# Partial sums of exponentials in a two-layer attention trunk: two tiles a head instead of four, one group of ones products for both heads

## The chip, the cores and the metric

The kernel runs on one core of a Trainium2 chip. The metric is the device time of one execution in microseconds (us); lower is better. The core has five engines that the profile names by short names: PE (TensorE, matrix products; PEld is its loading of weights), DVE (VectorE), ACT (ScalarE), POOL (GpSimd) and SP (SyncE, which issues the DMAs). Every engine works through its own queue in order, and semaphores make one engine wait for another.

## The reference, cut to what matters

There are two layers. Each projects a normalised input (1024 latent tokens and 256 context tokens, 1024 features), runs attention and a linear recurrence side by side, and merges the two. The change is in the attention:

```python
def gqa(q, k, v):
    s = jnp.einsum('bqkgd,bskd->bkgqs', q, k).astype(jnp.float32)
    p = jax.nn.softmax(s, axis=-1).astype(v.dtype)
    return jnp.einsum('bkgqs,bskd->bqkgd', p, v)
...
    k_all = jnp.concatenate([k_c, k_l], axis=1)
    v_all = jnp.concatenate([v_c, v_l], axis=1)
    o_lat = latent_attention(q_l, k_all, v_all)
...
    if need_ctx:
        o_ctx = gqa(q_c.reshape(B, L, N_KV_HEADS, Q_PER_KV, HEAD_DIM), k_c, v_c).reshape(B, L, D_ATTN)
```

There are 16 query heads of 64 features. A latent query sees all 1280 keys, a context query only the 256 context keys. Layer 0 needs the context rows too, layer 1 doesn't. The softmax's denominator, the sum of the exponentials over the keys, is what the changed lines compute.

## The kernel before

Activations lie with features on the 128 partitions and tokens along the row. Tokens come in three chunks: L0 and L1 of 512 latent tokens, C of 256 context tokens. A product in full precision is split: each operand is a high part (fp32r) and the rest, and three fast products stand for one.

The attention of a layer is cut into **units**. A tile `t` of 0 to 7 holds two heads. For each tile there are four latent units, (L0, head 0), (L0, head 1), (L1, head 0), (L1, head 1), and in layer 0 a fifth, C, which takes both heads at once (256 queries each). A latent unit has 512 queries and ten key tiles (`kt`) of 128 keys, a context unit two. So there are 32 latent units in each layer and 8 context units in layer 0. In a unit:

- `s1` multiplies queries by keys once for the row maxima; VectorE reduces each result (`mp`, line 979).
- `s2`, for each key tile, makes the scores again, transposed (keys on the partitions), with the maximum subtracted by an extra row. ScalarE takes the exponential twice, as fp32 (`pf`, line 1006) and as fp32r (`ph`, line 1007). VectorE makes the rest `pl = pf - ph` (line 1008), which reads two tiles in SBUF.
- `add` sums the `pf` tiles on GpSimd into partial tiles `acc` (lines 1019, 1022, 1024). The ten key tiles of a latent unit make four partial tiles, by the groups (0,1,2), (3,4,5), (6,7), (8,9). The first member of a group needs no instruction, so a latent unit has six additions. A context unit copies its two tiles into two partial tiles.
- `av` multiplies `ph` and `pl` by the values (`avps`).
- `lsum` multiplies the partial tiles by a tile of ones that is 32 columns wide (`lps`). Product x fills partitions 32x to 32x+31 of one bank. ScalarE copies the bank (`lrow`), and one DMA writes one row of each product to DRAM (`ls`).
- `recip`, after the second head, reads the partial sums of both heads back from DRAM spread over 128 partitions, adds them on VectorE (lines 1080 and 1082, `rq`), takes the reciprocal, and sends it through DRAM to the partitions where `done` scales the output.

`acc` has five buffers, `pf` three, `pl` four. The bank that `s1`, `s2`, `lps` and the fills use is one of six.

PE's order is the order in which the Python code calls `mm`. A clock of the builder, `tl.now`, grows with every product by its supposed cost, and the steps of the units are due at times of that clock: the list of steps is stretched over the time that the units (`cost`) and the **fills** (`fcost`) are supposed to take. Fills are the projections for the gates (`gps`), which run between the steps of the units, so that PE has work while the other engines make exponentials. A supposed cost only moves steps against each other in the order; nothing waits for the builder's clock on the chip. The other engines' orders follow from the same calls.

The ones products in fp32 are two instructions each in the trace, so that a group of four counts eight. The rows of the acc additions in the trace bear the lines 1022 (second member of a group) and 1024 (later ones).

Of the kernel before, what the change touches and what calls it, by code (L numbers as in the profile page):

```python
# [100 lines left out]
def trunk_kernel(ctx: ExitStack, tc: tile.TileContext, xT, cc, par, wmod, win, wgate, wo,  # L101
# [446 lines left out]
    def layer_dram(l):  # L548
# [7 lines left out]
        d["ls"] = {(t, c): dtile(l, f"ls{t}{c}", [4, 512] if c == "C" else [2, 4, 512]) for t in range(8) for c in och}  # L556
# [152 lines left out]
    for l in range(DEPTH):  # L709
# [206 lines left out]
        with tc.tile_pool(name="att", bufs=2, reuse_waits="tile") as work:  # L916
# [21 lines left out]
            zt = {}  # L938

            class Unit:  # L940


                def __init__(self, i, t, c, e, g0):
# [14 lines left out]
                    add(g0 + self.nkt + (5.0 if e == 2 else 3.6), self.lsum)  # L958
                    self.groups = ((0,), (1,)) if e == 2 else ((0, 1, 2), (3, 4, 5), (6, 7), (8, 9))
                    self.accs = {}  # L960
# [51 lines left out]
                def add(self, kt, pf):  # L1012

                    x = next(x for x, g in enumerate(self.groups) if kt in g)
                    at = self.groups[x].index(kt)
                    if at == 0:
                        self.accs[x] = pf
                        if self.e == 2:
                            G.tensor_scalar(self.acc_tile(x), pf, 1.0, 0.0, op0=OP.mult, op1=OP.add)
                    elif at == 1:  # L1020
                        first = self.accs[x]
                        G.tensor_add(self.acc_tile(x), first, pf)  # L1022
                    else:
                        G.tensor_add(self.accs[x], self.accs[x], pf)  # L1024

                def acc_tile(self, x):
                    self.accs[x] = work.tile([128, 512], F32, name="acc", tag="acc", bufs=5)
                    return self.accs[x]
# [21 lines left out]
                def lsum(self):  # L1050

                    lp = ptile("s", "lps")
                    ng = len(self.groups)
                    for x in range(ng):
                        mm(lp[32 * x:32 * x + 32], ones32, self.accs[x], True, True, 0.9 / ng)
                    row = sm("lrow")
                    S.activation(row[0:32 * ng], lp[0:32 * ng], AF.Copy)
                    ls = dd["ls"][self.t, self.c]
                    dst = ls if self.e == 2 else ls[self.e]
                    tl.at(1.2, lambda: DMA.dma_start(dst[0:ng], row[0:32 * ng:32]), True)  # L1060
                    if self.e:
                        tl.at(5.0, self.recip, True)

                def recip(self):
# [4 lines left out]
                    rq = const.tile([128, 40], F32, name="rq", tag="rq", bufs=2)  # L1069
# [8 lines left out]
                    def back():  # L1078
                        r = rq[:, 32:32 + x]
                        V.tensor_add(r, rs[:, 0], rs[:, 1])  # L1080
                        for y in range(2, ng):
                            V.tensor_add(r, r, rs[:, y])
# [258 lines left out]
```

## Time and profile before

| what | value |
|---|---|
| median of three runs | 3177.37 us |
| the profiled execution | 3176.29 us, span 3174.5 us, mean granted clock 0.984 |
| PE | 3049.5 us busy, 96% of the span |
| DVE | 2453.9 us, 77% |
| ACT | 1715.0 us, 54% |
| POOL | 1024.5 us, 32% |
| attention of layer 0 | from 598.9 to 1320.7 us of the span: 721.8 us |
| attention of layer 1 | from 2237.9 to 2882.6 us: 644.7 us |

The two stretches of attention run from the first `s1` product of a layer to the end of its last `lps` product. The busy time of PE is the union of modelled product times; since products are pipelined, one that is shown as 0.39 us long can be followed by the next after 0.23 us. The start of the next product tells what one costs.

### The profile page before, as it was taken

To read this page: it belongs to the slowest core of one execution; us is meant where nothing else is said; L and a number is where in the kernel's file an instruction comes from. 1 tells how busy PE (TensorE), PEld (TensorE's weight loads), DVE (VectorE), ACT (ScalarE), POOL (GpSimd) and SP (SyncE) were. 2 spreads that over 40 slices of the span, in tenths; PEclk is the share of its full clock that TensorE was granted. 3 is DMA by queue.
4 is the path that set the end of the run, shared out by engine and by line. 5 is a ranking of instruction groups with operands and counts; after the bars stand their busy time and mean duration, and the time that the engine had idled before them with its cause. 6 is when DMAs were issued, how large, how long until landed. Compare 5 with 4: busy or idle time off the path is not lost.

```text
span 3174.5 us, 42428 instructions
## 1 busy us (share of the span) xinstructions
PE 3049.5 (96%) x14592; PEld 2459.1 (77%) x14592; DVE 2453.9 (77%) x3675; ACT 1715.0 (54%) x3060; POOL 1024.5 (32%) x777
## 2 busy tenths in 40 slices
PE   7999999999999999999999999999999999999999
PEld 3788778788777777887777778777777777777887
DVE  7665887589989998556685776897799989996544
ACT  4323767466666666445654324676476666663222
POOL 0211444134334434245522222333244444441000
PEclk9999999999999999999999999999999999999999
DMA  5443111421222222254555452111412121115554
GB/s 197 145 149 126 44 57 50 125 63 54 76 68 82 60 62 75 97 189 158 170 196 175 135 176 71 58 47 53 123 55 76 58 75 58 55 58 173 183 173 140
DMA packets 243416, 332.08 MB, mean 105 GB/s; under 512 B 63664, under 2 KB 109552, under 8 KB 242944
## 3 DMA queue, kind: packets, MB, share of 16 engines
q1 hardware_dynamic: 243200, 329.37, 32.6%
q8 instruction: 115, 1.88, 0.2%
q14 instruction: 101, 0.83, 0.1%
HBM read 252.54 MB, written 76.58 MB: 104 GB/s over the span
## 4 chain that ended last, share of the span: by engine, by line
PE 53%; DVE 19%; issue 6%; ACT 4%; DMA 4%; POOL 3%; SPq 0%; DVEq 0%; POOLq 0%; ACTq 0%
PE gps L145 29%; PE avps L145 8%; PE s2ps L145 7%; PE s1ps L145 4%; DVE pl L1008 3%; DVE wlo L227 3%; DVE mp L979 2%; PE lps L145 2%; POOL macc L360 2%; PE gtps L145 1%; DVE ti L856 1%; PE qps L145 1%; POOL b L853 1%; DVE g L867 1%; PE vps L145 1%
## 5 line engine op out<-in xcount | busy, mean ns | idle before, releaser
L145 PE MATMUL gps<-h,whi 128*128 128x512 f32 x3328 | 1042.3, 394 | 18.3 <-DVE g L876 15.9
L145 PEld LDWEIGHTS gps<-h,whi 128*128 128x128 f32 x3328 | 613.5, 190 | 135.3 <-issue 10.7
L1008 DVE TENSOR_TENSOR pl<-pf,ph 128x512 fp32r<-128x512 f32 x656 | 627.2, 957 | 71.3 <-ACT ph L1007 67.9
L145 PE MATMUL gps<-h,wlo 128*128 128x512 f32 x1664 | 655.2, 394 | 1.4 <-DVE wlo L227 1.4
L1006 ACT ACTIVATE pf<-s2ps 128x512 f32<-128x512 f32 x656 | 392.9, 599 | 343.1 <-PE s2ps L145 171.7
L1022 POOL TENSOR_TENSOR acc<-pf 128x512 f32<-128x512 f32 x256 | 353.0, 1379 | 686.4 <-ACT pf L1006 686.2
L979 DVE TENSOR_REDUCE mp<-s1ps 128x1 f32<-128x512 f32 (+1 forms) x800 | 453.7, 584 | 59.9 <-PE s1ps L145 56.5
L1007 ACT ACTIVATE ph<-s2ps 128x512 fp32r<-128x512 f32 x656 | 390.0, 595 | 0.0
L227 DVE TENSOR_TENSOR wlo<-wraw,whi 128x512 fp32r<-128x512 f32 x392 | 330.8, 865 | 62.2 <-ACT whi L226 33.0
L226 ACT ACTIVATE whi<-wraw 128x512 fp32r<-128x512 f32 x324 | 194.6, 628 | 340.9 <-PE gps L145 269.1
L145 PEld LDWEIGHTS gps<-h,wlo 128*128 128x128 f32 x1664 | 314.3, 189 | 71.4 <-DVE wlo L227 2.2
L145 PE MATMUL s1ps<-k,qa 128*128 128x512 f32 (+1 forms) x800 | 287.3, 368 | 15.9 <-DMA qa<-q0L 10.7
L145 PEld LDWEIGHTS s1ps<-k,qa 128*128 128x128 f32 x800 | 244.5, 310 | 55.4 <-DVE mp L979 10.6
L145 PE MATMUL avps<-pl,vv 128*128 128x512 f32 x656 | 262.4, 400 | 8.0 <-DVE pl L1008 7.7
L145 PE MATMUL avps<-ph,vv 128*128 128x512 f32 x656 | 266.2, 406 | 0.0
L145 PE MATMUL s2ps<-qa,k 128*128 128x512 f32 x656 | 260.8, 398 | 4.4 <-DVE mp L979 3.4
L145 PE MATMUL s2ps<-qb,k 65*128 65x512 f32 x656 | 262.5, 400 | 0.1
L145 PE MATMUL gps<-e,whi 128*128 128x512 f32 x768 | 244.8, 399 | 0.4 <-DVE e L227 0.2
L360 POOL TENSOR_TENSOR macc<-macc,wmt 128x512 f32<-128x512 f32 x112 | 156.6, 1398 | 252.3 <-ACT wmt L358 228.0
L1024 POOL TENSOR_TENSOR acc<-acc,pf 128x512 f32<-128x512 f32 x128 | 183.1, 1430 | 79.4 <-ACT pf L1006 77.4
L145 PE MATMUL qps<-h,whi 128*128 128x512 f32 x640 | 203.6, 399 | 1.7 <-DVE h L674 0.9
L145 PE MATMUL gps<-c,whi 128*128 128x256 f32 x1024 | 197.8, 289 | 2.7 <-DVE c L222 1.9
(214 smaller groups left out, 4945.0 us busy)
## 6 DMA issues: line engine op xcount, KB each, us to landing
wraw<-in_win_dram SPq DMA_DIRECT2D x200, 256.0 KB
wraw<-in_wo_dram SPq DMA_DIRECT2D x192, 256.0 KB
wm<-in_wmod_dram SPq DMA_DIRECT2D x32, 512.0 KB
wm<-in_wmod_dram SPq DMA_DIRECT2D x8, 1024.0 KB
rb<-rq SPq DMA_DIRECT2D x64, 128.0 KB
k<-k SPq DMA_DIRECT2D x24, 320.0 KB
v<-vst SPq DMA_DIRECT2D x20, 256.0 KB
vv<-v SPq DMA_DIRECT2D x8, 640.0 KB
```

Source lines behind the costliest of these rows:

```text
L145: nc.tensor.matmul(o, a, b, start=start, stop=stop)
L226: S.activation(dst_hi, src, AF.Copy)
L227: (V if lo_eng == "v" else G).tensor_sub(dst_lo, src, r32(dst_hi))
L360: G.tensor_add(acc, acc, t)
L853: G.tensor_mul(a2, a2, ti)
L856: V.tensor_tensor_scan(h, a, a2, 0.0, op0=OP.mult, op1=OP.add)
L979: tl.at(0.3, lambda: V.reduce_max(self.mp[:, j, b:b + 1], ps[:, :n], axis=AX.X))
L1006: S.activation(pf, ps, AF.Exp)
L1007: S.activation(ph, ps, AF.Exp)
L1008: tl.at(1.4, lambda: V.tensor_sub(pl, pf, r32(ph)))
L1022: G.tensor_add(self.acc_tile(x), first, pf)
L1024: G.tensor_add(self.accs[x], self.accs[x], pf)
```

## The change

A latent unit now has two partial tiles, by the groups (0,1,2,3,4) and (5,6,7,8,9), so it has eight additions on GpSimd instead of six. The partial tiles of head 0 are kept until head 1 has made its own, and one `lsum` after head 1 multiplies all four by ones: one group of four products, one `lrow`, one DMA to DRAM for the two heads of a tile and chunk. A context unit adds its two tiles into one partial tile and makes one product. `recip` adds two rows of partial sums for each head instead of four; for a context unit there is nothing to add. The builder's clock counts 1.1 for a group (before 0.9) and 0.58 for each latent unit in `cost` (before 0.9).

```diff
-        d["ls"] = {(t, c): dtile(l, f"ls{t}{c}", [4, 512] if c == "C" else [2, 4, 512]) ...}
+        d["ls"] = {(t, c): dtile(l, f"ls{t}{c}", [1, 512] if c == "C" else [4, 512]) ...}
...
-                    add(g0 + self.nkt + (5.0 if e == 2 else 3.6), self.lsum)
-                    self.groups = ((0,), (1,)) if e == 2 else ((0, 1, 2), (3, 4, 5), (6, 7), (8, 9))
-                    self.accs = {}
+                    if e:
+                        add(g0 + self.nkt + (5.0 if e == 2 else 3.6), self.lsum)
+                    self.groups = ((0, 1),) if e == 2 else ((0, 1, 2, 3, 4), (5, 6, 7, 8, 9))
+                    if e != 1:
+                        sums[t, c] = []
+                    self.sums, self.acc = sums[t, c], None
...
-                    x = next(x for x, g in enumerate(self.groups) if kt in g)
-                    at = self.groups[x].index(kt)
+                    at = next(g.index(kt) for g in self.groups if kt in g)
                     if at == 0:
-                        self.accs[x] = pf
-                        if self.e == 2:
-                            G.tensor_scalar(self.acc_tile(x), pf, 1.0, 0.0, op0=OP.mult, op1=OP.add)
+                        self.acc = pf
                     elif at == 1:
-                        first = self.accs[x]
-                        G.tensor_add(self.acc_tile(x), first, pf)
+                        first = self.acc
+                        self.acc = work.tile([128, 512], F32, name="acc", tag="acc", bufs=5)
+                        G.tensor_add(self.acc, first, pf)
+                        self.sums.append(self.acc)
                     else:
-                        G.tensor_add(self.accs[x], self.accs[x], pf)
+                        G.tensor_add(self.acc, self.acc, pf)
...
-                    ng = len(self.groups)
-                    for x in range(ng):
-                        mm(lp[32 * x:32 * x + 32], ones32, self.accs[x], True, True, 0.9 / ng)
+                    ng = len(self.sums)
+                    for x, acc in enumerate(self.sums):
+                        mm(lp[32 * x:32 * x + 32], ones32, acc, True, True, 1.1 / ng)
...
-                        V.tensor_add(r, rs[:, 0], rs[:, 1])
-                        for y in range(2, ng):
-                            V.tensor_add(r, r, rs[:, y])
-                        V.reciprocal(r, r)
+                        if ng == 2:
+                            V.tensor_add(r, rs[:, 0], rs[:, 1])
+                        V.reciprocal(r, r if ng == 2 else rs[:, 0])
...
-                    cost += (4 * 0.108 + 2 * 0.864 + 0.9 if ctxu else 4 * 0.54 + 10 * 0.864 + 0.9)
+                    cost += (4 * 0.108 + 2 * 0.864 + 0.9 if ctxu else 4 * 0.54 + 10 * 0.864 + 0.58)
```

On PE, the first `lps` group of the kernel before stands after head 0 of tile 0, chunk L0, with four partial tiles of that head; a second group for head 1 comes 82 products later.

```order
L145 MATMUL s1ps_5874<-k1_5130,qa_5689 128x256
L145 MATMUL lps_5876<-acc_5607,ones32_89 32x512
L145 MATMUL lps_5876<-acc_5670,ones32_89 32x512
L145 MATMUL lps_5876<-acc_5742,ones32_89 32x512
L145 MATMUL lps_5876<-acc_5787,ones32_89 32x512
L145 MATMUL avps_5862<-ph_5823,vv_5136 128x512
```

In the changed kernel the first group on PE stands where head 1's stood, between steps of the unit that follows, and its four tiles are two of head 0 and two of head 1.

```order
L145 MATMUL s1ps_6085<-k1_5130,qa_5907 128x256
L145 MATMUL lps_6088<-acc_5603,ones32_89 32x512
L145 MATMUL lps_6088<-acc_5709,ones32_89 32x512
L145 MATMUL lps_6088<-acc_5823,ones32_89 32x512
L145 MATMUL lps_6088<-acc_5933,ones32_89 32x512
L145 MATMUL avps_6073<-ph_6038,vv_5136 128x512
```

So the group after head 0 is gone from PE's queue, and the one after head 1 stays. On POOL, the first latent unit of the kernel before is these six additions.

```order
L1022 TENSOR_TENSOR acc_5607<-pf_5571,pf_5595 128x512
L1024 TENSOR_TENSOR acc_5607<-acc_5607,pf_5616 128x512
L1022 TENSOR_TENSOR acc_5670<-pf_5642,pf_5662 128x512
L1024 TENSOR_TENSOR acc_5670<-acc_5670,pf_5683 128x512
L1022 TENSOR_TENSOR acc_5742<-pf_5708,pf_5731 128x512
L1022 TENSOR_TENSOR acc_5787<-pf_5756,pf_5776 128x512
```

The same unit on POOL in the changed kernel has eight (its lines are 1023 for a group's second member and 1026 for later ones).

```order
L1023 TENSOR_TENSOR acc_5603<-pf_5565,pf_5583 128x512
L1026 TENSOR_TENSOR acc_5603<-acc_5603,pf_5613 128x512
L1026 TENSOR_TENSOR acc_5603<-acc_5603,pf_5635 128x512
L1026 TENSOR_TENSOR acc_5603<-acc_5603,pf_5657 128x512
L1023 TENSOR_TENSOR acc_5709<-pf_5677,pf_5701 128x512
L1026 TENSOR_TENSOR acc_5709<-acc_5709,pf_5723 128x512
L1026 TENSOR_TENSOR acc_5709<-acc_5709,pf_5746 128x512
L1026 TENSOR_TENSOR acc_5709<-acc_5709,pf_5768 128x512
```

Key tiles 3 and 8, which had begun a group and needed nothing, now each have an addition; so has key tile 6, while key tile 5 has lost its own. Around the first context unit, POOL's queue before holds the end of the last latent unit of tile 0, the two copies, and the first additions of tile 1.

```order
L1022 TENSOR_TENSOR acc_6431<-pf_6398,pf_6421 128x512
L1022 TENSOR_TENSOR acc_6485<-pf_6445,pf_6474 128x512
L1019 TENSOR_SCALAR acc_6507<-pf_6493 128x512
L1019 TENSOR_SCALAR acc_6530<-pf_6522 128x512
L1022 TENSOR_TENSOR acc_6571<-pf_6539,pf_6560 128x512
```

After the change the same place on POOL reads so.

```order
L1026 TENSOR_TENSOR acc_6389<-acc_6389,pf_6424 128x512
L1026 TENSOR_TENSOR acc_6389<-acc_6389,pf_6445 128x512
L1023 TENSOR_TENSOR acc_6507<-pf_6475,pf_6495 128x512
L1023 TENSOR_TENSOR acc_6548<-pf_6519,pf_6540 128x512
L1026 TENSOR_TENSOR acc_6548<-acc_6548,pf_6568 128x512
```

The context unit takes the fifth `acc` buffer while the four of the latent pair wait for their products; the addition that finds no free buffer is now the first of the next tile (acc_6548), where it was the second copy (acc_6530).

## Rows read from the trace of the kernel before

**Rows 1.** The page: busy time and share, and the chain that ended last.
```profile
PE 3049.5 (96%) x14592; PEld 2459.1 (77%) x14592; DVE 2453.9 (77%) x3675; ACT 1715.0 (54%) x3060; POOL 1024.5 (32%) x777
...
PE gps L145 29%; PE avps L145 8%; PE s2ps L145 7%; PE s1ps L145 4%; DVE pl L1008 3%; DVE wlo L227 3%; DVE mp L979 2%; PE lps L145 2%; POOL macc L360 2%; PE gtps L145 1%; DVE ti L856 1%; PE qps L145 1%; POOL b L853 1%; DVE g L867 1%; PE vps L145 1%
```

**Rows 2.** Windows, both attentions: length, busy of PE, PEld, DVE, ACT, POOL, clock, DMA.
```profile
598.90:1320.70 721.80, 715.00 (x3387) 571.29 (x3387) 627.51 (x1021) 459.89 (x893) 278.07 (x210) 1.00 0.24 69
2237.90:2882.60 644.70, 631.55 (x2788) 496.00 (x2788) 596.88 (x908) 422.78 (x807) 274.65 (x194) 0.99 0.22 66
```

**Rows 3.** Timeline of PE round a group of four: start, length.
```profile
1080.58 0.40 PE L145 MATMUL gps<-h,wlo 128*128 128x512 f32 x1
1080.81 0.28 PE L145 MATMUL s1ps<-k,qa 128*128 128x256 f32 x1
1081.03 1.06 PE L145 MATMUL lps<-acc,ones 128*32 128x512 f32 x8
1082.02 0.50 PE L145 MATMUL avps<-ph,vv 128*128 128x512 f32 x1
1082.36 0.40 PE L145 MATMUL avps<-pl,vv 128*128 128x512 f32 x1
```

**Rows 4.** The same, round a context unit's group of two.
```profile
718.96 1.05 PE L145 MATMUL lps<-acc,ones 128*32 128x512 f32 x4
719.94 0.50 PE L145 MATMUL s2ps<-qa,k 128*128 128x512 f32 x1
```

**Rows 5.** Timeline of DVE and POOL in layer 1, two additions and three subtractions.
```profile
2301.73 1.29 POOL L1022 TENSOR_TENSOR acc<-pf 128x512 f32<-128x512 f32 x1 [2.57 <-ACT pf L1006]
2302.17 1.40 DVE L1008 TENSOR_TENSOR pl<-pf,ph 128x512 fp32r<-128x512 f32 x1 [0.33 <-ACT ph L1007]
...
2305.05 0.69 DVE L1008 TENSOR_TENSOR pl<-pf,ph 128x512 fp32r<-128x512 f32 x1
...
2308.64 0.98 DVE L1008 TENSOR_TENSOR pl<-pf,ph 128x512 fp32r<-128x512 f32 x1
...
2309.28 1.49 POOL L1024 TENSOR_TENSOR acc<-acc,pf 128x512 f32<-128x512 f32 x1 [0.21 <-ACT pf L1006]
```

**Rows 6.** Groups by form, DVE, attention of layer 0: count, busy, mean ns, idle before.
```profile
L1008 DVE TENSOR_TENSOR pl<-pf,ph 128x512 fp32r<-128x512 f32 x336 | 314.6, 937 | 51.9 <-ACT ph L1007 49.9
L979 DVE TENSOR_REDUCE mp<-s1ps 128x1 f32<-128x512 f32 x256 | 171.4, 680 | 27.3 <-PE s1ps L145 26.4
```

**Rows 7.** The same in the attention of layer 1.
```profile
L1008 DVE TENSOR_TENSOR pl<-pf,ph 128x512 fp32r<-128x512 f32 x320 | 312.6, 977 | 19.4 <-ACT ph L1007 18.0
```

**Rows 8.** Windows of the `acc` tiles alone: length, busy of PE, PEld, POOL.
```profile
598.90:1320.70 721.80, 42.48 (x288) 6.39 (x288) 275.75 (x208) 1.00 0.24 69
2237.90:2882.60 644.70, 34.04 (x256) 5.15 (x256) 272.33 (x192) 0.99 0.22 66
```

**Rows 9.** Groups by form, DVE, whole span: the additions of partial sums.
```profile
L1082 DVE TENSOR_TENSOR rq<-rq 128x8 f32<-128x8 f32 x64 | 22.6, 354 | 1.5
...
L1080 DVE TENSOR_TENSOR rq<-rq 128x4 f32<-128x4 f32 x8 | 1.2, 146 | 4.6 <-DMA rq<-ls7C 4.6
```

**Rows 10.** Windows within layer 1's attention: the fullest and the loosest.
```profile
2300.00:2400.00 100.00, 98.84 (x449) 77.64 (x447) 98.39 (x153) 70.54 (x136) 45.66 (x32) 1.00 0.20 59
2500.00:2600.00 100.00, 94.73 (x411) 72.97 (x410) 93.47 (x144) 65.14 (x125) 43.10 (x31) 0.98 0.26 77
```

**Rows 11.** Timeline of PE in layer 1: a wait for a subtraction.
```profile
2555.23 0.39 PE L145 MATMUL avps<-ph,vv 128*128 128x512 f32 x1
2557.64 0.50 PE L145 MATMUL avps<-pl,vv 128*128 128x512 f32 x1 [2.02 <-DVE pl L1008]
```

**Rows 12.** Waits, layer 0's attention: us in total, times, longest.
```profile
POOL acc L1019 <- PE lps L145: 45.7, 8, 6.5
```

**Rows 13.** Groups, ACT, whole span: the copies of the ones products.
```profile
L1057 ACT ACTIVATE lrow<-lps 128x512 f32<-128x512 f32 (+1 forms) x72 | 43.1, 599 | 43.0 <-PE lps L145 40.3 <-ACT whi L226 0.3
```

More of the change, by code (lines that the diff above doesn't have):

```diff
@@ L555, in layer_dram @@
         d["za"] = {(t, c): dtile(l, f"za{t}{c}", [128, CH[c][1]]) for t in range(8) for c in och}
-        d["ls"] = {(t, c): dtile(l, f"ls{t}{c}", [4, 512] if c == "C" else [2, 4, 512]) for t in range(8) for c in och}
+        d["ls"] = {(t, c): dtile(l, f"ls{t}{c}", [1, 512] if c == "C" else [4, 512]) for t in range(8) for c in och}
         d["l"] = {(t, c): dtile(l, f"l{t}{c}", [2, CH[c][1]]) for t in range(8) for c in och}
@@ L936, in add @@
                 ev.append((g, cnt[0], fn))
-            zt = {}
+            zt, sums = {}, {}
             class Unit:
@@ L1052, in lsum @@
                     lp = ptile("s", "lps")
-                    ng = len(self.groups)
-                    for x in range(ng):
-                        mm(lp[32 * x:32 * x + 32], ones32, self.accs[x], True, True, 0.9 / ng)
+                    ng = len(self.sums)
+                    for x, acc in enumerate(self.sums):
+                        mm(lp[32 * x:32 * x + 32], ones32, acc, True, True, 1.1 / ng)
                     row = sm("lrow")
                     S.activation(row[0:32 * ng], lp[0:32 * ng], AF.Copy)
[L1058 to L1062, printed above, removed]
+                    tl.at(1.2, lambda: DMA.dma_start(dd["ls"][self.t, self.c], row[0:32 * ng:32]), True)
+                    tl.at(5.0, self.recip, True)
                 def recip(self):
@@ L1068, in recip @@
                     ng, x = len(self.groups), n // 64
-                    rq = const.tile([128, 40], F32, name="rq", tag="rq", bufs=2)
+                    rq = const.tile([128, 24], F32, name="rq", tag="rq", bufs=2)
                     rs = rq[:, 0:ng * x].rearrange("p (s x) -> p s x", s=ng)
                     if self.e == 2:
-                        DMA.dma_start(rs, ls[0:ng].rearrange("s (p x) -> p s x", p=128))
+                        DMA.dma_start(rs, ls.rearrange("s (p x) -> p s x", p=128))
                     else:
                         for e in range(2):
-                            DMA.dma_start(rs[64 * e:64 * e + 64], ls[e].rearrange("s (p x) -> p s x", p=64))
+                            DMA.dma_start(rs[64 * e:64 * e + 64], ls[2 * e:2 * e + 2].rearrange("s (p x) -> p s x", p=64))
                     rl = sm("rl")
                     def back():
-                        r = rq[:, 32:32 + x]
-                        V.tensor_add(r, rs[:, 0], rs[:, 1])
-                        for y in range(2, ng):
-                            V.tensor_add(r, r, rs[:, y])
-                        V.reciprocal(r, r)
+                        r = rq[:, 16:16 + x]
+                        if ng == 2:
+                            V.tensor_add(r, rs[:, 0], rs[:, 1])
+                        V.reciprocal(r, r if ng == 2 else rs[:, 0])
                         tl.at(0.5, lambda: DMA.dma_start(ld.rearrange("e (p x) -> (e p) x", p=64), r), True)
```

3 lines of the change are left out of this document (removed).

## The prediction

> **What bounds the kernel now.** I read the page first, then the two attention stages by windows, since nothing outside them is touched. The page says that PE is busy for 96% of the span and DVE for 77%, and the chain that ended last is PE for the most part, with the ones products at 2% and the subtraction `pl` at 3% [rows 1]. An average over stages hides the tight one. By windows, layer 0's attention lasts 721.8 us with DVE busy for 627.5, a share of 86.9%, and layer 1's lasts 644.7 us with DVE busy for 596.9, 92.6% [rows 2]. PE's idle time, by the modelled ends, is 721.8 - 715.0 = 6.8 us in layer 0 and 644.7 - 631.6 = 13.1 us in layer 1. So PE sets the pace in both, and DVE is close behind it, closest in layer 1. There the loosest 100 us have DVE 93.5% busy and PE only 94.7%, though another 100 us run with DVE at 98.4% and PE at 98.8% [rows 10]: DVE's load hurts PE where it comes in bunches. One such place is a wait of PE for a subtraction, 2.02 us long [rows 11].
>
> **What PE loses.** A group of four ones products starts at 1081.03 and the next product at 1082.02: 0.99 us. There is more at its edges. The product behind it has 0.34 us to the next start, where an ordinary one has 0.23 (1080.58 to 1080.81): 0.11 more. The product ahead, with 256 columns, should take half of 0.23 and takes 0.22 (1080.81 to 1081.03): 0.10 more [rows 3]. Together 1.20 us. Of 64 latent groups (32 in each layer) half go, 16 in a layer: 16 x 1.20 = 19.2 us of PE's work in each layer, 38.4 us in all.
>
> Is the price one of the group or of each product? A context unit's group of two takes 719.94 - 718.96 = 0.98 us [rows 4], as good as the 0.99 of four. So products of a group run beside each other, the group is what costs, and I take nothing for the context units, whose group of two becomes one product. No row shows a group of one. If it took half of 0.98, eight of them would give 4 us more; if it took longer than a group of two, for which no row gives a reason, it would be a few tenths each.
>
> **What ACT and SP lose.** ACT makes 32 copies `lrow` less, at 0.599 us [rows 13] 19 us. It is busy for 460 and 423 us of the two stages [rows 2] and doesn't set the pace; I count nothing. SP issues 32 writes and 32 reads or so less, which lie on no engine's path.
>
> **What DVE loses.** The second and third addition of partial sums go (64 instructions, 22.6 us: their mean is 354 ns), and the first one of the eight context units (1.2 us) [rows 9]. That is 23.8 us, about 12 in layer 0 and 11 in layer 1.
>
> **What POOL gains, and what DVE pays for it.** A latent unit has eight additions where it had six, a context unit one where it had two copies: in layer 0 from 208 to 264 instructions, in layer 1 from 192 to 256. POOL's time for them is now 275.8 and 272.3 us [rows 8]; at 1.4 us for a further addition it rises by some 80 and 90 us, to little over half of each stage [rows 2]. POOL itself can take this. But additions and subtractions get in each other's way. With POOL quiet a subtraction takes 0.69 us. One that began at 2302.17, while an addition ran from 2301.73 to 2303.02, took 1.40 us and ended 0.55 after the addition. In the other direction, the addition of 2309.28 began while a subtraction ran until 2309.62, and took 1.49 us instead of 1.29 [rows 5]. The reduction `mp`, which reads a bank of PSUM, keeps 680 ns on average [rows 6].
>
> The Trainium skill speaks of this, and against the change: the page "SBUF — State Buffer", in "Who interferes with whom", says that a VectorE instruction with two SBUF inputs and a GpSimd instruction that reads SBUF share a port pair, and that the one that starts first holds it for its whole length while the other fully blocks. The rows just told agree. By that rule alone an extra addition can cost DVE the length of an addition, 1.29 us, which as an estimate would be 64 x 1.29 = 83 us in layer 1; at 98.4% of DVE that stage would take (597 - 11 + 83) / 0.984 = 680 us, and the kernel about 3193. The slower rival below is this case at the price of the rows.
>
> By the rows, the mean subtraction takes 937 ns in layer 0 [rows 6] and 977 in layer 1 [rows 7]. Over 690 that is 336 x 0.247 = 83 us and 320 x 0.287 = 92 us, or 0.40 and 0.48 us for each of the 208 and 192 instructions of POOL [rows 8]. The extra 56 and 64 would cost 22 and 31 us at this price. The upper bound is the full wait of the row above, 1.40 - 0.69 = 0.71 us each: 40 and 45 us. The lower bound is nothing: additions that follow each other closely begin behind a subtraction and run while DVE reduces, which takes no wait. I take half of the mean price, 11 and 16 us, since DVE, as full as it is here, comes to many subtractions late, when the addition is nearly over (the one at 2308.64 took 0.98, a wait of 0.29 [rows 5]), and a fuller DVE comes later still.
>
> **What PE does with it.** DVE's work is then 627.5 + 11 - 12 = 626.5 us in layer 0, and 596.9 + 16 - 11 = 602 in layer 1. If PE kept all of its gain the stages would last 702.6 and 625.5 us, and DVE's share would be 89% and 96%. In layer 0 that is still below the 92.6% of layer 1 today, where PE idles 2.0% against 0.9% in layer 0; some 3 us of more idle time leave 16 of the 19. In layer 1, DVE at its fullest share of 98.4% could do 602 us in 612, so that all would be kept; at today's mean of 92.6% it would need 650, and nothing would be kept. I take the middle between 625.5 and 644.7, rounded to the careful side: 8 us kept. Together 24 us: the profiled execution, 3176.3 us, becomes 3152, and the median of the runs, 1 us above it, 3153.
>
> **Edits that I cost at nothing.** The builder's clock counts 0.35 us less for a latent unit (0.9 once, now 1.1 for two), and `cost` 0.32 less, so that steps and fills keep their ratio. The pair's four tiles are kept for two units in five buffers. POOL waited 45.7 us in eight places for the ones products of the pair at a context unit's second copy [rows 12]; this wait moves to the first addition of the next tile, two key tiles later, and should get shorter. It is hidden as long as the three `pf` buffers last; queued behind the waiting addition are POOL's next additions, and the exponential of the next but two key tiles waits for them. Should all of the seven such places lose 1 us on PE, it is 7 us.
>
> **Rivals.** *All is kept.* If additions in a row fit between subtractions, DVE's work falls by the 24 us of additions that go, and PE keeps 38.4 us: 3139. For it speaks the 98.4% of [rows 10]; against it the waits of PE for subtractions [rows 11], which a fuller DVE makes no rarer.
>
> *DVE takes it all.* At the mean price of an addition, DVE's work is 627.5 + 22 - 12 = 638 us and 596.9 + 31 - 11 = 617. If its share can rise no further than today's, layer 1 takes 617 / 0.926 = 666 us, 21 more, and layer 0, whose share has room up to the same 92.6%, loses up to 19: 3177, no change. PE's freed time would be idle time.
>
> *The additions cost more than the products.* At the full wait, DVE's work is 597 + 45 - 11 = 631 us in layer 1; at a share of 92.6% it takes 681 us, 37 more. Layer 0 would have 627.5 + 40 - 12 = 656 us of DVE in 708, 14 less. That gives 3177 - 14 + 37 = 3200. It decides from the point where the extra wait in layer 1 makes that stage longer by what layer 0 gains: at the share of today, 25 to 29 us of wait, 0.39 to 0.45 us for each extra addition. That is about the mean price, where this case and the one before it meet; both take a DVE that can't be filled further, which the fullest window speaks against.
>
> That the change *doesn't do what it says* can be ruled out for the count of instructions; what could fail is the early release of `acc`, of which the 7 us above are the price.
>
> **Chances.** My forecast 0.50, all kept 0.20, no change 0.15, slower (3200) 0.13, another cause 0.02. The likeliest time is 3153. The range from 3136 to 3182 takes in the first three and a few us for the context products and the spread of runs, and leaves out 0.15 or so. 2% are 64 us, about what a measurement of this kernel can tell from no change. No case reaches that: faster by over 2% 0.01, slower by over 2% 0.02, within 2% 0.97.
>
> **What the changed profile would show.** Ones products: 272 instructions instead of 544, 40 groups, each still about 0.98 to 1.0 us to the next product; a context group shorter than 0.9 would say that products count. POOL's additions 264 and 256. The mean of the subtractions tells the cases apart: about 0.97 in layer 0 and 1.03 in layer 1 for my forecast, no longer than now for all kept, 1.06 and 1.12 for the slower case. The stages: 706 and 637 us for mine, 703 and 626 for all kept, 681 in layer 1 for the slower one. I am wrong if layer 0 keeps less than 10 us, or if layer 1 gets longer, or if the time between the attentions, which I take as untouched, moves by more than 5 us.

## The result, and the profile after

The change makes the kernel slower by half a per cent. The median is 3188.86 us against 3172.35 us, ratio 1.0051 with a 95% interval from 1.0035 to 1.0067; the same file run again (`again`, below) gives 1.0042, from 1.0030 to 1.0055. The forecast was 3153 us, with a range up to 3182. The first profile of the changed kernel fell into a disturbed execution, so all rows of it here are from the run `again`, whose profiled execution has a span of 3189.6 us.

The page of the changed kernel: busy times, and the chain that ended last.

```profile
PE 3032.0 (95%) x14320; PEld 2450.2 (77%) x14320; DVE 2510.7 (79%) x3603; ACT 1694.9 (53%) x3028; POOL 1216.2 (38%) x897
...
PE gps L145 15%; DVE pl L1011 4%; DVE mp L982 2%; PE avps L145 2%; PE s2ps L145 2%; DVE wlo L227 2%; PE s1ps L145 1%; PE qps L145 1%; DVE ti L856 1%; PE gtps L145 1%; PE vps L145 1%; DVE ti L860 0%; DVE rq L1076 0%; DVE z L1046 0%; DVE g L867 0%
```

PE has 17.5 us less busy time than in [rows 1], less than half of the 38.4 us that the prediction took off. That is no measure of the products' gain, since the busy time holds some waiting: with the same 3246 products in layer 0's attention PE is busy for 705.4 us here and for 692.1 in `two_adds` (below). DVE has 57 us more, though the change takes instructions from it. An addition of partial sums 8 elements wide (`rq`) has come into the list of the chain, though with less than half a per cent.

The two attention stages of the changed kernel by windows, columns as in [rows 2].

```profile
598.40:1322.70 724.30, 705.37 (x3246) 568.62 (x3246) 661.12 (x979) 448.38 (x876) 378.49 (x266) 1.00 0.22 68
2246.00:2899.50 653.50, 628.47 (x2669) 492.38 (x2669) 622.43 (x880) 415.41 (x794) 366.32 (x258) 0.99 0.21 65
```

Layer 0's stage is 724.3 us long, 2.5 more than in [rows 2], and layer 1's 653.5, 8.8 more. DVE is busy for 661.1 (+33.6) and 622.4 us (+25.5). These 11.3 us are not all of the 15.1 us between the two profiled executions. The time between the two attentions, in which nothing was edited, grew by 6.1 us, from 917.2 (1320.7 to 2237.9) to 923.3 (1322.7 to 2246.0); the two ends took 2.3 us less. By the traces' clock records the granted clock stood at its lower level, 1.2 GHz, for 64.2 us of that stretch here and for 54.6 in the kernel before, which at half the clock can make up to 4.8 of the 6.1 us. The other eight traces with eight additions a unit have 915.3 to 922.0 us there, so the change doesn't set this figure. A stage of one execution can be off by some us in the same way.

The products do cost what was read in [rows 3]:

```profile
2314.78 0.28 PE L145 MATMUL s1ps<-k,qa 128*128 128x256 f32 x1
2314.99 1.06 PE L145 MATMUL lps<-acc,ones 128*32 128x512 f32 x8
2315.99 0.50 PE L145 MATMUL avps<-ph,vv 128*128 128x512 f32 x1
2316.32 0.39 PE L145 MATMUL avps<-pl,vv 128*128 128x512 f32 x1
```

A group is 1.00 us to the next product, with 0.33 behind that. There are 32 latent groups in place of 64. A context unit's group is a single product now, the case for which the prediction had no row:

```profile
717.51 1.04 PE L145 MATMUL lps<-acc,ones 128*32 128x512 f32 x2
718.49 0.50 PE L145 MATMUL s2ps<-qa,k 128*128 128x512 f32 x1
```

The eight of them take 0.97 to 0.98 us to the next product. One product costs what two and four do.

DVE's groups by form in layer 0's stage, then in layer 1's, to be read against [rows 6, 7, 9].

```profile
L1011 DVE TENSOR_TENSOR pl<-pf,ph 128x512 fp32r<-128x512 f32 x336 | 342.7, 1022 | 35.1 <-ACT ph L1010 33.0 <-PE avps L145 0.6
L982 DVE TENSOR_REDUCE mp<-s1ps 128x1 f32<-128x512 f32 x256 | 170.8, 680 | 22.2 <-PE s1ps L145 21.2
...
L227 DVE TENSOR_TENSOR wlo<-wraw,whi 128x512 fp32r<-128x512 f32 x37 | 40.6, 1113 | 4.4 <-ACT whi L226 4.4
...
L1076 DVE TENSOR_TENSOR rq<-rq 128x8 f32<-128x8 f32 x15 | 11.4, 761 | 0.0
```

```profile
L1011 DVE TENSOR_TENSOR pl<-pf,ph 128x512 fp32r<-128x512 f32 x320 | 336.8, 1053 | 10.6 <-ACT ph L1010 9.3
...
L227 DVE TENSOR_TENSOR wlo<-wraw,whi 128x512 fp32r<-128x512 f32 x38 | 34.4, 918 | 2.3 <-ACT whi L226 2.3
...
L1076 DVE TENSOR_TENSOR rq<-rq 128x8 f32<-128x8 f32 x15 | 15.5, 1033 | 0.0
```

Subtractions take 1.02 and 1.05 us, 28 and 24 us more in all. The subtraction of the weights' split, `wlo`, also reads two tiles in SBUF. In the kernel before it had these two rows, in the stages of layer 0 and layer 1:

```profile
L227 DVE TENSOR_TENSOR wlo<-wraw,whi 128x512 fp32r<-128x512 f32 x38 | 29.0, 771 | 3.5 <-ACT whi L226 2.9 <-PE s2ps L145 0.4
```

```profile
L227 DVE TENSOR_TENSOR wlo<-wraw,whi 128x512 fp32r<-128x512 f32 x36 | 27.0, 754 | 1.5 <-ACT whi L226 1.5
```

So it costs 12 and 7 us more. And the additions of partial sums, over the whole span of the changed kernel and of the kernel before (its first additions of a pair; the later ones are in [rows 9]):

```profile
L1076 DVE TENSOR_TENSOR rq<-rq 128x8 f32<-128x8 f32 x32 | 27.2, 851 | 4.9 <-DMA rq<-ls7L 4.9
```

```profile
L1080 DVE TENSOR_TENSOR rq<-rq 128x8 f32<-128x8 f32 x32 | 6.1, 191 | 4.8 <-DMA rq<-ls7L 4.8
```

Before there were 104 such additions, 22.6 + 1.2 + 6.1 = 29.9 us. Now there are 32, and they take 27.2: one of 128 by 8 takes 0.85 us on average. The timeline shows why. The first line is one with no addition beside it on POOL, the other two are one that meets an addition:

```profile
764.84 0.15 DVE L1076 TENSOR_TENSOR rq<-rq 128x8 f32<-128x8 f32 x1
...
852.31 1.29 POOL L1026 TENSOR_TENSOR acc<-acc,pf 128x512 f32<-128x512 f32 x1 [0.41 <-ACT pf L1009]
...
852.37 1.25 DVE L1076 TENSOR_TENSOR rq<-rq 128x8 f32<-128x8 f32 x1
```

Of the 32, 25 met an addition on POOL, and each of these ended 0.02 to 0.03 us after that addition. The other seven took 0.15 to 0.17 us. The reduction `mp`, with its one operand in PSUM, keeps its 680 ns.

POOL's additions, by windows of the `acc` tiles as in [rows 8], and the waits for subtractions and maxima in layer 1's stage:

```profile
598.40:1322.70 724.30, 25.41 (x144) 3.66 (x144) 376.17 (x264) 1.00 0.22 68
2246.00:2899.50 653.50, 17.00 (x128) 2.52 (x128) 364.00 (x256) 0.99 0.21 65
```

```profile
PEld avps L145 <- DVE pl L1011: 32.3, 58, 2.2
...
PE avps L145 <- DVE pl L1011: 12.5, 20, 1.9
PEld s1ps L145 <- DVE mp L982: 11.4, 20, 1.6
PEld s2ps L145 <- DVE mp L982: 10.6, 20, 2.2
```

The same waits in the kernel before:

```profile
PEld avps L145 <- DVE pl L1008: 14.6, 22, 2.3
...
PEld s1ps L145 <- DVE mp L979: 7.8, 9, 1.7
PE avps L145 <- DVE pl L1008: 6.8, 8, 2.0
...
PEld s2ps L145 <- DVE mp L979: 2.9, 8, 0.6
```

PE waits 58 times for a subtraction before it can load weights, where it waited 22 times. Places like that of [rows 11] have become common.

### The profile page after: what moved, and what is told of

Read it like the earlier page. It is cut to its first block, busy times and chain, and to the rows that moved or that the text cites. A ratio compares the mean times of both kernels' runs of the same rounds, so it can differ in the third digit from the quotient of the medians.

```text
span 10304.0 us, 42105 instructions
## 1 busy us (share of the span) xinstructions
PE 10290.6 (100%) x14320; PEld 5857.0 (57%) x14320; DVE 2487.7 (24%) x3603; ACT 1732.6 (17%) x3028; POOL 1091.0 (11%) x897
## 4 chain that ended last, share of the span: by engine, by line
PE 100%; DVE 0%; ACT 0%; DMA 0%; issue 0%
PE gps L145 56%; PE avps L145 11%; PE s2ps L145 10%; PE qps L145 9%; PE s1ps L145 5%; PE gtps L145 4%; PE vps L145 2%; PE modps L145 1%; PE lps L145 1%; PE ssq L145 0%; PE rb L145 0%; PE ssn L145 0%; PE modpt L341 0%; DMA par<-in_par_dram 0%; ACT qg L467 0%; DVE spt L206 0%
## 5 line engine op out<-in xcount | busy, mean ns | idle before, releaser
L145 PE MATMUL gps<-h,whi 128*128 128x512 f32 x3328 | 3193.2, 1094 | 0.0
L145 PEld LDWEIGHTS gps<-h,whi 128*128 128x128 f32 x3328 | 1429.4, 435 | 1162.8 <-issue 1155.4
L145 PE MATMUL gps<-h,wlo 128*128 128x512 f32 x1664 | 1817.4, 1092 | 0.0
L145 PE MATMUL s1ps<-k,qa 128*128 128x512 f32 (+1 forms) x800 | 744.5, 946 | 0.0
L145 PE MATMUL gps<-e,whi 128*128 128x512 f32 x768 | 739.1, 1099 | 0.0
L145 PE MATMUL s2ps<-qb,k 65*128 65x512 f32 x656 | 724.3, 1104 | 0.0
L145 PE MATMUL s2ps<-qa,k 128*128 128x512 f32 x656 | 722.3, 1101 | 0.0
L145 PE MATMUL avps<-pl,vv 128*128 128x512 f32 x656 | 720.0, 1098 | 0.0
L145 PE MATMUL avps<-ph,vv 128*128 128x512 f32 x656 | 717.0, 1093 | 0.0
L145 PEld LDWEIGHTS gps<-c,whi 128*128 128x128 f32 x1024 | 476.7, 511 | 100.3 <-issue 97.6
```

The lines of the kernel that those rows point to most:

```text
L145: nc.tensor.matmul(o, a, b, start=start, stop=stop)
```

## The experiments

The first theory was that GpSimd's additions hold up VectorE's two-input instructions, and that this takes more than the products give. The second was that the builder's clock, which the change also sets anew, moved steps so that TensorE waits. Ratios are to the kernel before, with 95% intervals.

### again

No edit. 

> The changed kernel itself, once more, for a trace in which its stages can be read. First theory (additions on GpSimd block VectorE's subtractions, and more of them cost more than half of the ones products give back): the mean subtraction is 1.06 us or more in layer 0 and 1.12 or more in layer 1, VectorE is busy for over 95% of layer 1's attention, and that stage is longer than 644.7 us by 15 to 30 us, while layer 0's is about as long as before. Second theory (the builder's clock, 1.1 and 0.58 in place of 0.9, has moved steps against each other, and TensorE waits for the steps): subtractions stay at 0.94 and 0.98 us, and TensorE's waits are for scores or maxima.

1.0042 (1.0030 to 1.0055), with the rows above. Subtractions are at 1.02 and 1.05 us, less than the first theory wanted and far from the second's 0.94 and 0.98. Layer 1's stage is 9 us longer, not 15 to 30, and layer 0's 2.5. VectorE's share of layer 1's stage, 95.2%, is as the first theory wanted. One sign of the second is there too: PE's weight loads wait for maxima for 48.5 us in the two stages together, against 20.5 before. The run can't decide between the theories, since the lengthened subtractions stand in VectorE's queue ahead of the reductions.

### pool_only, pe_only: one half of the change at a time

```diff
 pool_only, on the changed kernel (with the builder's numbers of before):
-                    if e:
-                        add(g0 + self.nkt + (5.0 if e == 2 else 3.6), self.lsum)
+                    add(g0 + self.nkt + (5.0 if e == 2 else 3.6), self.lsum)
...
+                    dst = ls if self.e == 2 else ls[2 * self.e:2 * self.e + 2]
...
 pe_only, on the changed kernel:
-                    ... ((0, 1, 2, 3, 4), (5, 6, 7, 8, 9))
+                    ... ((0, 1, 2), (3, 4, 5), (6, 7), (8, 9))
-                        self.sums.append(self.acc)
+                        if kt < 5:
+                            self.sums.append(self.acc)
-                            V.tensor_add(r, rs[:, 0], rs[:, 1])
+                            V.scalar_tensor_tensor(r, rs[:, 0], 1.0, rs[:, 1], op0=OP.add, op1=OP.add)
```

> Eight additions on GpSimd for each latent unit as in the change, but a group of ones products after each head (two products each, 64 groups), and the builder's clock as before. First theory: the cost of the additions without the gain of the products, 30 to 40 us above the changed kernel, ratio to the kernel before 1.013 to 1.018. Second theory: the clock is the old one, so about the time before, 0.998 to 1.002.

> One group of four products for both heads and the clock of the change, but the six additions of before. Half of the partial tiles (those of key tiles 6 to 9) are left out of the sum, and 1 is added to it, so the output is not the reference's. First theory: the products' gain without the additions' cost, ratio 0.988 to 0.993 (24 to 38 us less than before). Second theory: the clock is that of the change, so slower than before like it, 1.003 to 1.006.

`pool_only` 1.0084 (1.0070 to 1.0099), `pe_only` 0.9930 (0.9917 to 0.9944). So eight additions in place of six cost 0.84%, 27 us, and half the groups give 0.70%, 22 us, when each is done alone. Both signs are the first theory's and against the second's. But both are smaller than the first theory expected: 1.0084 against 1.013 to 1.018, and 22 us against 24 to 38 (the ratio lies in its 0.988 to 0.993). Two products of a group, in `pool_only`, still take 0.98 us:

```profile
2313.02 1.05 PE L145 MATMUL lps<-acc,ones 128*32 128x512 f32 x4
2314.00 0.50 PE L145 MATMUL avps<-ph,vv 128*128 128x512 f32 x1
```

### two_adds, memsets: fewer additions, and work on GpSimd that reads nothing

```diff
 two_adds, on the changed kernel (with 1.0 added in recip as in pe_only):
-                    else:
-                        G.tensor_add(self.acc, self.acc, pf)
 memsets, on two_adds:
+                    else:
+                        junk = work.tile([128, 512], F32, name="acc", tag="acc", bufs=5)
+                        for _ in range(3):
+                            G.memset(junk, 0.0)
```

> The change with only the first addition of each group of five (two for a latent unit); key tiles 2 to 4 and 7 to 9 are left out of the sum, and 1 is added to it. First theory: subtractions fall to 0.75 to 0.85 us on average, TensorE keeps all of its gain and waits less, ratio 0.980 to 0.987. Second theory: as slow as the change, 1.003 to 1.006.

> As the run with two additions for a unit (the other six left out of the sum, 1 added to it), but in place of each addition left out GpSimd fills a tile with zeros three times, so that it is busy about as long as in the change, reading nothing. If it is GpSimd's reading of SBUF that holds VectorE up: subtractions near 0.80 us as with two additions, ratio 0.975 to 0.980. If it is that GpSimd is busy or late: subtractions over 0.95 us, ratio 0.990 to 1.006.

`two_adds` 0.9771 (0.9758 to 0.9785), `memsets` 0.9774 (0.9759 to 0.9788). These are the stages of `two_adds`, then of `memsets`, with length, PE, PEld, DVE, ACT and POOL:

```profile
598.00:1290.70 692.70, 692.05 (x3246) 569.90 (x3246) 567.30 (x979) 449.61 (x876) 102.17 (x74) 1.00 0.23 71
2210.70:2811.60 600.90, 599.48 (x2669) 492.40 (x2669) 530.37 (x880) 415.38 (x794) 99.43 (x66) 1.00 0.23 70
```

```profile
597.20:1290.90 693.70, 692.80 (x3246) 569.65 (x3246) 571.26 (x979) 449.50 (x876) 382.75 (x650) 1.00 0.23 71
2208.70:2809.60 600.90, 599.48 (x2669) 492.55 (x2669) 531.40 (x880) 415.14 (x794) 381.96 (x642) 1.00 0.23 70
```

`two_adds` gains more than the first theory's 0.980 to 0.987. `memsets` lies where it was expected if GpSimd's reading is the cause (0.975 to 0.980). GpSimd is busy for 382 us in layer 1 with memsets, more than the 366 of the changed kernel, and neither DVE nor the stage notices (530.4 and 531.4 us; 600.9 and 600.9). In layer 0 DVE has 4.0 us more and the stage 1.0. So it is not that GpSimd is busy. Is it that GpSimd is late, and keeps the `pf` buffers that ScalarE needs? These are ScalarE's longest waits for that in `memsets`, in layer 0 and in layer 1:

```profile
ACT pf L1009 <- POOL acc L1028: 19.3, 23, 1.1
```

```profile
ACT pf L1009 <- POOL acc L1028: 9.9, 12, 1.1
```

As the profile assigns them, all its waits for `pf` behind GpSimd come to 20.2 and 12.4 us there, against 0.9 and 1.6 in `two_adds`, and the stages are as long; in the changed kernel they are 34.2 and 20.0. (`late_add`, below, has far longer ones at no cost.) What is left is that an addition reads SBUF and a memset doesn't. (A memset is also shorter, 0.53 us against 1.29 for an addition that meets nothing.)

With the same groups of products and the same builder's numbers, the ratio is 0.9771 for two additions a unit, 0.9930 for six (`pe_only`) and 1.0042 for eight. The stages of `pe_only`:

```profile
599.80:1307.50 707.70, 700.07 (x3246) 567.74 (x3246) 623.19 (x979) 450.02 (x876) 282.45 (x202) 1.00 0.23 70
2226.10:2862.20 636.10, 616.92 (x2669) 493.99 (x2669) 594.45 (x880) 415.34 (x794) 272.60 (x194) 0.99 0.21 66
```

This gives the price of an addition on VectorE, all its instructions counted. From two to six additions (128 more in each layer) DVE's busy time rises by 55.9 and 64.1 us, 0.44 and 0.50 us for each. From six to eight (64 more) it rises by 37.9 and 28.0 us, 0.59 and 0.44. The subtractions of `two_adds` fall to 0.80 us in layer 0 and 0.81 in layer 1; this is layer 0's row:

```profile
L1011 DVE TENSOR_TENSOR pl<-pf,ph 128x512 fp32r<-128x512 f32 x336 | 269.3, 802 | 81.0 <-ACT ph L1010 76.5 <-PE avps L145 2.3
```

`two_adds` also shows how long PE's own work is at most, since PE idles for only 0.7 and 1.4 us there: about 692 and 600 us with the change's groups. The changed kernel's stages are 32 and 54 us longer than that.

### late_add: an addition waits for its own subtraction

```diff
-                    tl.at(1.0, lambda: self.add(kt, pf))
+                    tl.at(1.45, lambda: self.add(kt, pf))
...
+                    if at:
+                        G.tensor_scalar(pf[:, 0:1], pf[:, 0:1], 1.0, 0.0, op0=OP.mult, op1=OP.add)
                     if at == 0:
```

> The change, with an instruction of one column on GpSimd ahead of each addition that rewrites pf's first column, so that an addition cannot start before the subtraction of its own key tile has read pf. If most of the cost is the addition that starts 0.6 us ahead of its own subtraction: subtractions fall to 0.75 to 0.90 us, ratio 0.990 to 0.999. If an addition then only meets the next key tile's subtraction, or holds pf too long: subtractions stay above 1.0 us, ratio 1.003 to 1.010.

1.0038 (1.0024 to 1.0051): as the change. The first of the two readings was wrong, the second holds. Subtractions are at 1.03 and 1.08 us. In layer 1's stage GpSimd now waits for subtractions, and ScalarE for the `pf` buffers that the late additions hold:

```profile
POOL pf L1019 <- DVE pl L1011: 208.0, 214, 37.7
ACT pf L1009 <- POOL acc L1028: 106.4, 124, 2.7
ACT pf L1009 <- POOL acc L1025: 72.9, 58, 2.6
PEld avps L145 <- DVE pl L1011: 42.4, 71, 2.2
```

Layer 1's subtractions are no shorter, so a later addition must meet another one; no timeline is shown for it. ScalarE's 179.2 us of waits for `pf` behind GpSimd, nine times the 20.0 of the changed kernel, left the time where it was. The rewriting instruction itself, 0.28 us each, is part of this run's cost, so the run doesn't give the price of the position alone.

### rq_pool, before_rq: the additions of partial sums on GpSimd

```diff
-                            V.tensor_add(r, rs[:, 0], rs[:, 1])
+                            G.tensor_add(r, rs[:, 0], rs[:, 1])
```

> The change, with the addition of the two partial sums (128 by 8, 0.85 us on VectorE in the trace of the changed kernel) on GpSimd. First theory (blocked VectorE paces the stage): VectorE loses 27 us of work in both layers and the time falls by 8 to 20 us, ratio 0.998 to 1.002. Second theory (the builder's clock): no change from 1.004 to 1.005.

> The kernel before with the three additions of partial sums on GpSimd in place of VectorE, where they take 30 us in all. If VectorE's blocked time is what TensorE waits for in the kernel before too: 0.995 to 0.998. If TensorE alone sets its pace: 0.999 to 1.001.

On the changed kernel 1.0014 (1.0004 to 1.0025), 2.8 thousandths or 9 us less than the change; on the kernel before, where all three additions move, 0.9974 (0.9963 to 0.9984). Both lie where the first theory wanted them, near its slower end. But VectorE did not lose its 27 us on the changed kernel. Its busy time over the whole span fell by 8.1 us, from 2510.7 to 2502.6: the subtractions grew to 1.04 and 1.07 us and took back half of what had gone. On the kernel before it fell by 26.0 us, from 2453.9 to 2427.9. So moving these tiny instructions was worth 8 to 9 us in either kernel, for very different amounts of VectorE's time; `old_clock_rq` below shows that the gain does not hold in every order.

### old_clock, mid_clock, slow_clock, slower_clock: the builder's numbers

```diff
-                        mm(lp[32 * x:32 * x + 32], ones32, acc, True, True, 1.1 / ng)
+                        mm(lp[32 * x:32 * x + 32], ones32, acc, True, True, (0.9 if self.e == 2 else 1.8) / ng)
...
-  ... 4 * 0.54 + 10 * 0.864 + 0.58)
+  ... 4 * 0.54 + 10 * 0.864 + 0.9)
```

> The change with the builder's numbers of before: 1.8 for the group of a pair and 0.9 for a latent unit in the cost. First theory: as the change, 1.003 to 1.006. Second theory: the order is that of before again but for the products, ratio 0.990 to 0.999.

> The change with the builder's numbers half way between its own and those of before (1.45 for a group, 0.74 for a latent unit). If the time falls steadily as the clock counts more: 1.001 to 1.003, between 1.0042 and 0.9999. If the clock only deals the steps out anew, without a trend: anywhere from 0.997 to 1.006, and not in line with its neighbours.

> The change with larger numbers than before (2.1 for a group, 1.06 for a latent unit). If there is a trend: 0.995 to 0.999. Without a trend: from 0.997 to 1.006.

> The change with still larger numbers (2.45 for a group, 1.22 for a latent unit). If there is a trend: 0.991 to 0.997. Without a trend: from 0.997 to 1.006.

The numbers are those of a latent pair's group and of a latent unit. A context group counts 0.9 in the four new settings and 1.1 in the change.

| group, unit | ratio | interval |
|---|---|---|
| 1.1, 0.58 (the change) | 1.0042 | 1.0030 to 1.0055 |
| 1.45, 0.74 | 1.0037 | 1.0024 to 1.0051 |
| 1.8, 0.9 (as before) | 0.9999 | 0.9987 to 1.0011 |
| 2.1, 1.06 | 1.0013 | 1.0002 to 1.0025 |
| 2.45, 1.22 | 1.0019 | 1.0009 to 1.0030 |

The first theory expected 1.003 to 1.006 for `old_clock` and was wrong there: the numbers of before take back the whole loss, 14 us. The second theory, in its own terms (0.990 to 0.999), was wrong as well. And there is no steady trend: beyond the numbers of before the time falls no further, and the setting half way is hardly better than the change's own. With `old_clock` DVE is about as busy as in the changed kernel (658.0 and 618.0 us), in stages that are 6.5 and 8.4 us shorter:

```profile
597.80:1315.60 717.80, 703.91 (x3243) 566.84 (x3243) 657.98 (x980) 450.19 (x877) 384.79 (x266) 1.00 0.23 69
2233.40:2878.50 645.10, 618.59 (x2666) 489.69 (x2666) 618.01 (x880) 414.87 (x794) 376.47 (x258) 0.99 0.21 65
```

What differs is the wait for maxima. PE's weight loads wait for `mp` for 48.5, 44.5, 34.3, 41.5 and 40.8 us in the two stages, in the order of the table: by and large the slower settings have more of it. It goes the same way on the kernel before, with 20.5 us, and 14.7 with the change's numbers (`before_new_clock`, next). That is one execution of each, and whether the wait makes the difference was not tested. A small part can be the granted clock: behind the first 6 us of the stages it fell to half, for 3.4 us at a time, four times in the changed kernel and once in `old_clock`. Three such falls can lose some 5 us of work.

### pe_old_clock, before_new_clock: the clock with six additions

The same edits of numbers, on `pe_only` back to the old ones and on the kernel before to the new ones (0.55 for a group, 0.58 for a unit).

> Six additions, one group of products for a pair (half of the partial tiles left out of the sum, 1 added to it), with the builder's clock of before. Over the run with the clock of the change (0.993): if the clock's 14 us are lost whatever VectorE does, 0.987 to 0.990. If they are lost only where VectorE is full, 0.992 to 0.994.

> The kernel before with the builder's numbers of the change (0.55 for a group, 0.58 for a latent unit in the cost) and nothing else. If the clock alone costs: 1.003 to 1.006. If it costs only with eight additions: 0.999 to 1.001.

`pe_old_clock` 0.9924 (0.9912 to 0.9936), as `pe_only` and as the second of its expectations has it. `before_new_clock` 0.9969 (0.9957 to 0.9981): on the kernel before, the very numbers that cost the change 14 us gain 10. Neither of its expectations had that. So the numbers have no price of their own; each set deals the steps out in another order, and this is worth up to 0.4% either way. With six additions and half the groups the two settings tried agree.

With the old numbers in all four corners, the halves of the change can be compared without this: six additions and all groups 1, eight additions and all groups 1.0084, six and half 0.9924, eight and half 0.9999. The products give 0.76 to 0.85%, 24 to 27 us, and the additions cost 0.75 to 0.84%, as much. They cancel. These prices hold for that setting. With the change's numbers three corners were run, 0.9969, 0.9930 and 1.0042; there half the groups give 0.39% and the additions cost 1.12%.

### old_clock_rq, before_new_clock_rq: do the gains add?

> The change with the builder's clock of before and the addition of the two partial sums on GpSimd. If the two gains add (4.3 thousandths for the clock, 3.0 for the addition): 0.996 to 0.998, the fastest of those that compute the whole sum. If they are two ways to the same waits: 0.999 to 1.001.

> The kernel before with the builder's numbers of the change and the three additions of partial sums on GpSimd. If the two gains add (3.1 and 2.6 thousandths): 0.993 to 0.996. If both shorten the same waits: 0.996 to 0.998.

They don't: 0.9998 (0.9989 to 1.0008) and 0.9976 (0.9965 to 0.9987), no faster than `old_clock` and `before_new_clock` alone. In `old_clock_rq` VectorE lost next to nothing by it: its busy time is 2502.6 us against 2503.8 in `old_clock`. The fastest that computes the whole sum are the two edits of the kernel before, `before_new_clock` at 0.9969, 3165.55 us, and `before_rq` at 0.9974. Both beat both kernels; neither needs the change.

## Why the prediction was wrong

The prediction added up 38.4 us from the products and took 14.4 of them off for VectorE. With the builder's numbers of before, the products alone are worth 24 to 27 us, the additions alone cost as much, and the change comes out level. Its own numbers, which the prediction put at nothing, make it 14 us slower. All three signs of being wrong that the prediction names came up in the traces: layer 0 kept nothing, layer 1 got longer, and the time between the attentions moved by 6.1 us.

**What PE loses** was right in its price: a group still costs 1.00 us to the next product, one or two products cost what four do, and the count of groups halved. The 19.2 us for each layer were not measured by themselves. Taking them, with 692 and 600 us as PE's own work after the change (the windows of `two_adds`), PE's idle time was about 10 and 25 us before and is 32 and 54 after. The stages grew by 2.5 and 8.8 us, so all 19.2 us saved in each layer came back as waits, and these on top.

**What DVE loses** failed. I took 24 us off DVE for 72 additions of partial sums, since their rows said so [rows 9]. But much of those rows was wait: one that meets nothing takes 0.15 to 0.17 us, and the later ones of 128 by 8 took 0.35 on average [rows 9]. The 32 that remain took over the waits and cost 27.2 us in place of 6.1, so that DVE lost 2.7 us, not 24. An instruction 8 elements wide waits for the end of an addition as one of 512 does.

**What POOL gains, and what DVE pays for it** is the step that failed most, by its size. The mechanism was told rightly from [rows 5], and `memsets` bears it out. I priced it at 11 and 16 us, half of the mean, on the argument that a fuller DVE comes later to its subtractions. The subtractions alone measured 28 and 24 us more, 0.50 and 0.38 us for each added instruction, about the mean price (0.40 and 0.48) that I had halved. And I counted subtractions alone: `wlo` added 12 and 7 us, and `rq` did not go. DVE rose by 34 and 26 us where I had it fall by 1 and rise by 5.

The rule of the Trainium skill ("SBUF — State Buffer", "Who interferes with whom"), that the second of two such instructions fully blocks and that a GpSimd instruction that only writes doesn't contend, agrees with `memsets` and with the 25 additions of partial sums that ended 0.02 to 0.03 us behind an addition. The Trainium skill speaks there of VectorE instructions with two SBUF inputs and names no size.

I priced one kind of such instruction. The full 1.29 us for each addition, which the prediction gives as an estimate, was too high here: from six additions to eight (`pe_only` and the change), DVE's time rose by 0.59 and 0.44 us for each.

**What PE does with it** failed in both layers. I let DVE's share rise to 92.6% before PE should feel it in layer 0. It rose to 91.3%, and the stage lost its whole gain; so a share is no threshold. In layer 1 I took the middle between all and nothing, 8 us kept, and the stage grew by 8.8. That PE waits where instructions come in bunches fits its 58 waits for subtractions, but was not tested.

The result, 3189, lies half way between two of my rivals, "DVE takes it all" (3177) and "the additions cost more than the products" (3200). That is partly luck. Both have layer 0 gain 14 to 19 us and layer 1 lose 21 to 37; measured are a loss of 2.5 and one of 8.8. And without the builder's numbers, which neither counts, the time would be about the first one's. The price from which the second one decides, 0.39 to 0.45 us for each addition in layer 1, is about the 0.44 that all of VectorE's instructions make.

**The edit costed at nothing**, the builder's clock, was not nothing. With the old numbers the change measures 0.9999; with its own, 1.0042. That the change is slower and not just level is the doing of the order that these numbers make, together with eight additions. Shown is that it has no steady trend over five settings and that it turns round on the kernel before. Why one order is better than another, place by place, stays open; the waits for maxima go with it.

Two smaller points had no effect that shows. SP's reads of partial sums are 72 in both traces, not 32 fewer; its writes fell from 72 to 40. And the context units' single product cost as long as two, which the prediction had not counted as a gain.

The wait of POOL for a free `acc` buffer did get shorter, as said: 22.4 us in seven places, against the 45.7 of [rows 12].

```profile
POOL acc L1023 <- PE lps L145: 22.4, 7, 3.7
```

## What to carry to other kernels

Before work is moved to GpSimd, list every VectorE instruction of the stage with two SBUF inputs, the tiny ones too, and price each further GpSimd instruction that reads SBUF at no less than the mean wait that the trace shows already; here that was 0.4 to 0.5 us on the subtractions alone, and 0.44 to 0.59 us was measured with all of VectorE's instructions counted. Removing instructions whose row is mostly wait can remove little, because the wait moves to others: moving 27.2 us of them away in `rq_pool` took 8.1 us off VectorE. Where steps are dealt out by a builder's cost numbers, an edit that touches the numbers should be measured with the old ones as well: the order alone was worth 0.4% here, as much as the change, so that the prices of two halves of a change are no surer than that.

## What the runs showed that I had not expected

- 576 memsets in layer 1's stage, 382 us of GpSimd with the additions that were left, cost VectorE nothing (531.4 us against 530.4), while the 64 further additions of the change over the kernel before raised it by 26 us.
- An addition of 128x8 on VectorE took 0.85 us on average with eight GpSimd additions a unit, where the first ones of a pair before had taken 0.19 on average; 25 of 32 waited to the end of an addition.
- Holding an addition back until its own subtraction is done left the subtractions as long as they were (1.03 and 1.08 us).
- A builder's cost numbers, which add and remove no work, changed the time by 14 us, and by 10 us in the other direction in the kernel before.
